# A two-layer diffusion backbone on one core: MLP products in single PSUM banks taken in turn, dot products spread over both MLP products, two of four weight sums added by an accumulating DMA

## The chip, the cores and the metric

The kernel runs on one core of one Trainium2 chip. The time is the device time of one execution in microseconds (us), and lower is better. The core's engines are TensorE (PE, the matrix products, with PEld for its weight loads), VectorE (DVE), ScalarE (ACT), GpSimd (POOL) and SyncE (SP), which here only issues DMA transfers. TensorE writes its products into PSUM, which holds eight banks of 512 fp32 columns on 128 partitions; DVE and ACT read them from there.

## The reference, cut to what matters

```python
def sq_relu_mlp(h, w1, w2):
    return jnp.square(jax.nn.relu(h @ w1)) @ w2

def reference(...):
    h = ctx                                   # 256 context tokens; x: 512 latent tokens
    for l in range(2):
        mod_x = jax.nn.silu(c) @ w_ada[l] + b_ada[l]         # adaLN rows, 6 * 1024
        mod_c = jax.nn.silu(c_ctx) @ w_ada[l] + b_ada[l]
        ...                                                  # retention, attention, pooling
        x = x + g2 * sq_relu_mlp(modulate(rmsnorm(x, norm_mlp[l]), sh2, sc2), w_ff1[l], w_ff2[l])
        if not last:
            h = h + cg2 * sq_relu_mlp(modulate(rmsnorm(h, norm_mlp[l]), csh2, csc2), w_ff1[l], w_ff2[l])
    return rmsnorm(x, norm_final)
```

The model width is 1024, the MLP's inner width 4096. Everything is fp32. The change touches the MLP of both layers and, through it, the place of the adaLN products of layer 1.

## The kernel before

**Tokens and precision.** Activations lie transposed: features on the 128 partitions, tokens along the columns. Layer 0 has 768 columns (512 latent and 256 context tokens), layer 1 512 (latent alone). A matrix product is made of three matmuls on rounded parts (`mm3`, L206: high by high, high by low, low by high). So each 512-column piece of a weight is split after its load: ACT writes the rounded high part (L214), DVE the rest (L223). Both go into a tile `wt`. Pieces are split four ahead of the product that uses them.

**The MLP** is `layer_ff`. The inner width is cut into chunks, 8 in layer 0 and 4 in layer 1. A chunk has two stages. In the *ups*, columns of `w_ff1` give products `f` that ACT takes out of PSUM, with relu and square, into tiles `b` (L1409). DVE builds sums `T` of them (L1363, L1364) and splits all into tiles `act`. In the *downs*, blocks of `w_ff2` are multiplied by these. Except in the last chunk of a layer, the downs use the Strassen-Winograd scheme: of a block's four quarters A11, A12, A21 and A22 and their four sums S1 to S4, seven are multiplied by one activation tile each, in the order A11, S1, A12, S4, S3, S2, A22. A chunk has two such blocks in layer 0 (a product there has two output halves i = 0, 1 of 128 features with 6 matmuls each) and four in layer 1 (one output, 12 matmuls). The four sums are made by DVE out of the loaded quarters (`quarter`, L250), 128 by 512 elements each:

```python
a, b = {S1: (A21, A22), S2: (S1, A11), S3: (A11, A21), S4: (S2, A12)}[i]
```

There are 26 such blocks in the program: 2 in each of seven chunks of layer 0, 4 in each of three of layer 1. The last chunk of a layer is a plain product.

**What takes a product out of PSUM.** DVE, in two ways: `keep` adds it to a tile `V` in SBUF (L1363), `gate` multiplies it by the adaLN gate and adds it to the residual `x` (L1453). A11 needs both, S1, S3 and S2 a `keep`, A12, S4 and A22 gates.

**PSUM.** `psum(3, 2)` makes three tiles A of two banks each and two single banks B. In layer 0 each up and each product takes a whole tile A, so three are in flight, and a tile is free again when the last read of both its halves is done. In layer 1 `bank` hands out halves of the tiles A, so six products are in flight. The two banks B serve small products.

**The dots.** Part of the adaLN rows of layer 1 is not computed on PE: rows of the transposed `w_ada` (`w_adaT`, 256 KB each) are multiplied by the conditioning vector and summed by DVE instructions of 128 by 512 (L474, output and input `rows`; one or two for each load). 96 such loads belong to layer 0's MLP, spread over chunks 0 to 6, about 14 each. They are merged into the list of ups alone, not among the downs. Chunk 0 has more of this kind among its ups: 8 more row loads and a piece of layer 0's adaLN on PE (matmuls `ada<-rows`).

**What sets the order.** `layer_ff` writes a list of tasks, `emit` walks it: it starts the load of a weight 3 units, and that of a `rows` tile 8 tasks, before its use. All these loads stand in one row on the SP queue, and each waits there until its buffer is free: 4 buffers of 4 KB per partition for weights (a block of `w_ff2` takes two) and `N_RR` = 3 buffers for rows. Then a scheduler places the instructions of each engine; an engine runs its own in that order.

Of the kernel before, what the change touches and what calls it, by code (L numbers as in the profile page):

```python
# [15 lines left out]
P = 128  # L16
# [46 lines left out]
N_RR = 3  # L63
# [27 lines left out]
class Unit:  # L91
# [55 lines left out]
class Net:  # L147
    def __init__(self, nc, tc, es, a):
# [9 lines left out]
        self.ps = self.half = None  # L158
        self.es = es
# [82 lines left out]
    def quarter(self, u, i):  # L242

        if i < 4:
            return u.raw[i // 2][:, i % 2 * 512:i % 2 * 512 + 512]
        if i not in u.sums:
            a, b = {S1: (A21, A22), S2: (S1, A11), S3: (A11, A21), S4: (S2, A12)}[i]
# [1070 lines left out]
    def layer_ff(self, l, whole, groups):  # L1318
# [32 lines left out]
        def begin():  # L1351
            n = per * 2 // 4
            t = [self.d("V", F32).rearrange("p a t -> p (a t)") for _ in range(-(-3 // n))]
            for i, name in enumerate("U57"):
                st[name] = [t[i // n][:, (i % n * 4 + j) * hw:(i % n * 4 + j + 1) * hw] for j in range(4)]
                st[name, "all"] = t[i // n][:, i % n * 4 * hw:(i % n + 1) * 4 * hw].rearrange("p (j t) -> p j t", t=hw)
# [61 lines left out]
        def up(c, m, u):  # L1418
            if last:
                ps = self.bank("f1")  # L1420
                self.lin1(ps, u, H, NK, 0, w)
                evac(c, m, None, [(ps, 0, w)])
                return
            ps = self.A("f1", (P, 2, 512))
            for half in range(2):
                o = half * hw
                for k in range(NK):
                    s = slice(k * P, (k + 1) * P)
                    self.mm3(ps[:, half, :hw], u[:, 0, s], u[:, 1, s], H(k)[:, 0, o:o + hw], H(k)[:, 1, o:o + hw], k == 0, k == NK - 1)
                evac(c, m, half, [(ps[:, half, :hw], o, hw)])  # L1430
# [26 lines left out]
        def keep(c, blk, name, ps):  # L1457
            v = st[name, "all"][:, MP * blk:MP * blk + MP]
            if c == 0 and (name, blk) not in st:
                st[name, blk] = True  # L1460
# [4 lines left out]
        def gates(blk, ps, odd, half):  # L1465
            for i in range(MP):
                gate(2 * (MP * blk + i) + odd, half, ps[:, i, :], bool(odd))

        use = {A11: (B11, lambda c, j, ps: (keep(c, j, "U", ps), gates(j, ps, 0, 0))),
               S1: (T1, lambda c, j, ps: keep(c, j, "5", ps)),  # L1470
               A12: (B21, lambda c, j, ps: gates(j, ps, 0, 0)),
               S4: (B22, lambda c, j, ps: gates(j, ps, 0, 1)),
               S3: (T3, lambda c, j, ps: keep(c, j, "7", ps)),
               S2: (T2, lambda c, j, ps: keep(c, j, "U", ps)),
               A22: (T4, lambda c, j, ps: gates(j, ps, 1, 0))}

        def product(c, u, blk, name):
            q, f = use[name]
            ps = self.bank("f2")[:, None, :hw] if last else self.A("f2", (P, 2, 512))[:, :, :hw]
            t = u.pieces[name].t  # L1480
            for i in range(MP):
                for p in range(CP):
                    s = slice((i * CP + p) * P, (i * CP + p + 1) * P)
                    self.mm3(ps[:, i, :], t[:, 0, s], t[:, 1, s], *part(c, p, q), p == 0, p == CP - 1)
            f(c, blk, ps)

        def block(c, blk, u):
            cost = 3 * 4 * hw / 2.2
            return [Task(cost, lambda n=n: product(c, u, blk, n), (u.pieces[n],))
                    for n in (A11, S1, A12, S4, S3, S2, A22)]  # L1490
# [34 lines left out]
        for c in range(n_chunk):  # L1525
# [13 lines left out]
            extra = self.extra.pop(("ff1", l), []) if c == 0 else []  # L1539
# [202 lines left out]
```

## Time and profile before

| | us |
|---|---|
| median of 3 runs | 1658.56 (1658.44 to 1662.48) |
| the profiled execution | 1657.6 |
| its span in the trace | 1655.8 |
| PE busy in the span | 1552.9 (94%) |
| DVE busy | 1183.5 (71%) |
| ACT busy | 802.4 (48%) |

The profiled execution's time is 1.8 us longer than the span that its trace shows, and 1.0 us under the median. Busy times are those of one engine, and the engines work beside each other. In the rows further down, a number in square brackets is the time for which the engine stood idle before an instruction, with the instruction that ended this wait; PEclk is the clock that TensorE was granted, as a share of its full speed.

### The profile page before, as it was taken

Reading aid. Unit: us, or ns where it says so; the run is one execution under the profiler, and the core shown is the slowest. Engines: PE = TensorE matmul, PEld = TensorE weight load, DVE = VectorE, ACT = ScalarE, POOL = GpSimd, SP = SyncE. Lnnn points to the kernel's source line nnn. Section 1 sums busy time; section 2 is a strip of 40 time slices with the busy share of each in tenths; the row PEclk is TensorE's granted clock in tenths of the full one; section 3 lists DMA queues with packets and bytes.
Section 4 is the critical chain, followed back from the end, with each engine's and each line's share of the span. In section 5 each row is a group of like instructions: output and inputs, shape, how many; then the busy total and the mean of one; then the engine's idle time right before and its main releaser. Section 6 shows DMA issues by size and latency. Waiting matters only on the chain.

```text
span 1655.8 us, 24510 instructions
## 1 busy us (share of the span) xinstructions
PE 1552.9 (94%) x9100; PEld 1351.4 (82%) x9100; DVE 1183.5 (71%) x2564; ACT 802.4 (48%) x1635; POOL 38.2 (2%) x78
## 2 busy tenths in 40 slices
PE   5999999999869898999999998998999999999997
PEld 2898577878659798899988997976888788888976
DVE  5665756877787979779787948678556785867834
ACT  4425477545334343434434345267764655445443
POOL 0010000000000000000000000101000000000000
PEclk8999999999879899999999999999999999999999
DMA  9352545652433234332432231723433223242321
GB/s 368 112 150 64 148 103 127 193 188 84 128 114 109 96 108 133 116 121 96 131 112 84 88 109 63 208 80 86 101 103 121 77 89 103 71 121 73 119 89 51
DMA packets 69095, 191.98 MB, mean 116 GB/s; under 512 B 8944, under 2 KB 11504, under 8 KB 68976
## 3 DMA queue, kind: packets, MB, share of 16 engines
q1 hardware_dynamic: 65584, 180.18, 34.7%
q0 software_dynamic: 2816, 9.70, 2.6%
q8 instruction: 72, 1.18, 0.3%
q10 hardware_dynamic: 576, 0.52, 0.1%
q14 instruction: 47, 0.39, 0.1%
HBM read 159.97 MB, written 10.49 MB: 103 GB/s over the span
## 4 chain that ended last, share of the span: by engine, by line
PE 84%; DVE 10%; DMA 3%; ACT 3%; issue 1%; SPq 0%; DVEq 0%; ACTq 0%
PE f L206 48%; PE A L206 10%; PE sc L206 4%; PE oe L206 3%; PE pv L206 3%; PE res L206 3%; PE rv L206 2%; PE pT L1031 2%; PE ada L206 2%; DVE act L223 1%; DVE rows L474 1%; PE ro L206 1%; DMA rows<-w_adaT 1%; PE q L206 1%; DVE dot L474 1%; DMA raw<-w_ada 1%
## 5 line engine op out<-in xcount | busy, mean ns | idle before, releaser
L206 PE MATMUL f<-h,wt 128*128 128x384 f32 (+2 forms) x2400 | 466.9, 355 | 10.3 <-ACT b L1409 7.7
L206 PE MATMUL f<-act,wt 128*128 128x256 f32 (+2 forms) x2664 | 436.1, 324 | 41.2 <-DVE x L1453 15.3
L206 PEld LDWEIGHTS f<-h,wt 128*128 128x128 f32 x2400 | 419.9, 191 | 54.3 <-ACT b L1409 14.2
L206 PEld LDWEIGHTS f<-act,wt 128*128 128x128 f32 x2664 | 411.5, 195 | 64.1 <-DVE x L1453 17.2
L223 DVE TENSOR_TENSOR wt<-raw,wt 128x512 fp32r<-128x512 f32 x326 | 222.0, 687 | 150.5 <-ACT wt L214 148.1
L214 ACT ACTIVATE wt<-raw 128x512 fp32r<-128x512 f32 x326 | 201.4, 627 | 228.1 <-PE f L206 124.9
L206 PE MATMUL A<-h,wt 128*128 128x512 f32 (+2 forms) x864 | 171.9, 357 | 1.0 <-ACT h L554 0.5
L206 PEld LDWEIGHTS A<-h,wt 128*128 128x128 f32 x864 | 143.0, 190 | 27.5 <-ACT h L554 2.8
L214 ACT ACTIVATE wt<-sum 128x512 fp32r<-128x512 f32 x104 | 63.0, 628 | 154.2 <-DVE sum L250 143.0
L1409 ACT ACTIVATE b<-f 128x384 f32<-128x384 f32 (+2 forms) x98 | 50.5, 518 | 149.5 <-PE f L206 135.0
L206 PE MATMUL sc<-k,q 96*128 96x512 f32 (+1 forms) x384 | 85.5, 350 | 2.6 <-ACT p L1013 1.9
L474 DVE SCALAR_TENSOR_TENSOR rows<-rows,sbc 128x512 f32<-128x512 f32 x128 | 84.4, 686 | 1.9 <-DMA rows<-w_adaT 1.4
L206 PEld LDWEIGHTS sc<-k,q 96*128 96x128 f32 x384 | 62.8, 188 | 20.4 <-issue 5.5
L1363 DVE TENSOR_TENSOR V<-V,f 128x768 f32<-128x768 f32 (+1 forms) x86 | 62.5, 726 | 21.6 <-PE f L206 21.4
L223 DVE TENSOR_TENSOR wt<-sum,wt 128x512 fp32r<-128x512 f32 x104 | 70.6, 686 | 7.5 <-ACT wt L214 7.3
L1453 DVE SCALAR_TENSOR_TENSOR x<-f,mod,x 128x256 f32<-128x256 f32 (+2 forms) x148 | 68.9, 503 | 6.5 <-PE f L206 4.7
L1012 DVE TENSOR_REDUCE st<-sc 128x1 f32<-128x768 f32 x64 | 60.7, 953 | 15.1 <-PE sc L206 14.7
L1032 ACT ACTIVATE pT<-pT 128x384 f32<-128x384 f32 x128 | 56.5, 491 | 22.4 <-PE pT L1031 22.0
L214 ACT ACTIVATE act<-T 128x384 fp32r<-128x384 f32 (+1 forms) x104 | 47.6, 472 | 38.9 <-DVE T L1364 19.5
L223 DVE TENSOR_TENSOR act<-b,act 128x384 fp32r<-128x384 f32 (+2 forms) x94 | 47.5, 515 | 25.0 <-ACT act L214 24.9
L206 PE MATMUL res<-mix,wt 128*128 128x256 f32 (+1 forms) x384 | 59.1, 313 | 2.3 <-DVE om L1052 1.9
L1013 ACT ACTIVATE p<-sc,st 128x768 f32<-128x768 f32 x64 | 57.8, 905 | 5.6 <-DVE st L1012 4.4
(244 smaller groups left out, 1849.6 us busy)
## 6 DMA issues: line engine op xcount, KB each, us to landing
raw<-w_ff SPq DMA_DIRECT2D x128, 512.0 KB, 3.6
rows<-w_adaT SPq DMA_DIRECT2D x128, 256.0 KB, 3.0
raw<-w_in SPq DMA_DIRECT2D x22, 512.0 KB, 4.1
raw<-w_ada SPq DMA_DIRECT2D x16, 512.0 KB, 10.9
rows<-w_ada SPq DMA_DIRECT2D x32, 256.0 KB, 3.1
raw<-w_out SPq DMA_DIRECT2D x16, 512.0 KB, 3.7
x<-xd SPq DMA_DIRECT2D x6, 768.0 KB, 6.8
x<-xT SPq DMA_DIRECT2D x4, 768.0 KB, 6.5
```

The costliest lines, as they stand in the source:

```text
L206: self.nc.tensor.matmul(out, l, r, start=start, stop=stop)
L214: self.nc.scalar.activation(out, src, AF.Copy, **k)
L223: return self.nc.vector.tensor_tensor(out, src, hi.bitcast(F32), op=ALU.subtract)
L474: nc.vector.scalar_tensor_tensor(out, w, 1.0, self.sbc[:, v, half], op0=ALU.mult, op1=ALU.mult, accum_out=acc[:, v, i, j:j + 1])
L1012: nc.vector.tensor_reduce(st[:, 0:1], ps, axis=AX, op=ALU.max, negate=True)
L1013: nc.scalar.activation(p, ps, AF.Exp, bias=st[:, 0:1], accum_out=st[:, 1:2])
L1031: nc.tensor.transpose(ps[:, kt, :], p[:, (k0 + kt) * P:(k0 + kt + 1) * P], self.ident)
L1032: nc.scalar.activation(s["pT", h, qt // 2][:, k0:k0 + 3, c], ps, AF.Copy)
L1363: add = lambda x, y, z, op=ALU.add: nc.vector.tensor_tensor(x, y, z, op=op)
L1409: nc.scalar.activation(b[:, at:at + n], ps, AF.Relu)
L1453: self.mark = nc.vector.scalar_tensor_tensor(x, ps[:, at - o:at - o + n], g[:, cond:cond + 1], x, op0=ALU.mult, op1=ALU.add)
```

## The change

Four things change.

1. **Banks.** `bank` hands out all eight banks in turn: the two halves of a tile A, a bank B, two halves, a B, two halves. Ups and products of both layers take one bank for each half (`up`) or for each output half i (`product`). A product of layer 0 becomes two tasks, and its `keep` two additions of 128 by 384 in place of one of 128 by 768.
2. **Sums.** The order of the quarters in `w_ff2` becomes A21, A22, A11, A12. A block is loaded by three DMAs on the SP queue in place of two: A21 twice, side by side into the tile `sums` (512 KB written), A11 and A12 into `raw` (512 KB), and A22 into half a tile `rh` (256 KB, two buffers). Then a DMA on the POOL queue adds A22 and A11, from HBM, to what lies in `sums` (512 KB): the tile then holds S1 and S3. DVE makes S2 and S4 alone. In a plain chunk A21 is loaded once and nothing is added.
3. **Dots.** They are merged into ups and downs together; in chunk 0 among the downs alone, since its ups keep the other rows.
4. **Room.** `N_RR` goes from 3 to 2, the descriptor memory of software DMAs from 4096 to 2048.

```diff
 def bank(self, name):
-    if self.half is None:
+    i = self.turn
+    self.turn = (i + 1) % 8
+    if i in (2, 5):
+        return self.B([P, 512], name)
+    if i in (0, 3, 6):
         self.half = self.A(name, (P, 2, 512))
         return self.half[:, 0, :]
-    t, self.half = self.half, None
-    return t[:, 1, :]
+    return self.half[:, 1, :]
...
 def load_unit(self, u):
         if u.kind == "st":
-            u.raw = [self.wr.tile([P, UW], F32, tag="r", name=self.nm("raw")) for _ in range(2)]
-            for i in range(2):
-                q.dma_start(u.raw[i], u.ap[:, i * 1024:i * 1024 + 1024])
+            u.raw = [self.wr.tile([P, UW], F32, tag="r", name=self.nm(n)) for n in ("sums", "raw")]
+            u.raw.append(self.wr.tile([P, 512], F32, tag="rh", name=self.nm("raw"), bufs=2))
+            r = u.raw[0].rearrange("p (a c) -> p a c", a=2)
+            if u.plain:
+                q.dma_start(r[:, 0, :], u.ap[:, 0:512])
+            else:
+                q.dma_start(r, u.ap[:, None, 0:512].to_broadcast([P, 2, 512]))
+            q.dma_start(u.raw[1], u.ap[:, 1024:2048])
+            q.dma_start(u.raw[2], u.ap[:, 512:1024])
+            if not u.plain:
+                self.nc.gpsimd.dma_start(u.raw[0], u.ap[:, 512:1536], accum_op=ALU.add)
             return
...
-            a, b = {S1: (A21, A22), S2: (S1, A11), S3: (A11, A21), S4: (S2, A12)}[i]
+            a, b = {S2: (S1, A11), S4: (S2, A12)}[i]
...
-        def product(c, u, blk, name):
+        def product(c, u, i, j, name):
             q, f = use[name]
-            ps = self.bank("f2")[:, None, :hw] if last else self.A("f2", (P, 2, 512))[:, :, :hw]
+            ps = self.bank("f2")[:, :hw]
             t = u.pieces[name].t
-            for i in range(MP):
-                for p in range(CP):
-                    s = slice((i * CP + p) * P, (i * CP + p + 1) * P)
-                    self.mm3(ps[:, i, :], t[:, 0, s], t[:, 1, s], *part(c, p, q), p == 0, p == CP - 1)
-            f(c, blk, ps)
+            for p in range(CP):
+                s = slice((i * CP + p) * P, (i * CP + p + 1) * P)
+                self.mm3(ps, t[:, 0, s], t[:, 1, s], *part(c, p, q), p == 0, p == CP - 1)
+            f(c, j, ps)
...
-            extra = self.extra.pop(("ff1", l), []) if c == 0 else []
             share = -(-len(spread) // max(n_chunk - 1 - c, 1))
-            extra, spread = extra + spread[:share], spread[share:]
-            out += merge(ups, extra)
...
+            extra, spread = spread[:share], spread[share:]
+            if c == 0:
+                out += merge(ups, self.extra.pop(("ff1", l), []))
+                out += merge(downs, extra)
+            else:
+                out += merge(ups + downs, extra)
```

How the order moves is shown at three places. The first is PE at the start of the downs of layer 0's chunk 3, just after the last up. `f_1196` is the product A11, `f_1198` S1, `f_1202` A12 and `f_1204` S4; a row with x3 is three matmuls. Before:

```order
L206 MATMUL f_1196_6697<-act_6514,wt_6532 128x384
L206 MATMUL f_1198_6716<-act_6394,wt_6537 128x384 x3
L206 MATMUL f_1198_6716<-act_6598,wt_6537 128x384 x3
L206 MATMUL f_1198_6716<-act_6394,wt_6537 128x384 x3
L206 MATMUL f_1198_6716<-act_6598,wt_6537 128x384 x3
L206 MATMUL f_1202_6737<-act_6474,wt_6608 128x384 x3
L206 MATMUL f_1202_6737<-act_6598,wt_6608 128x384 x3
L206 MATMUL f_1202_6737<-act_6474,wt_6608 128x384 x3
L206 MATMUL f_1202_6737<-act_6598,wt_6608 128x384 x3
L206 MATMUL f_1204_6755<-act_6474,wt_6615 128x384 x3
L206 MATMUL f_1204_6755<-act_6675,wt_6615 128x384 x3
```

Now, from the same place on: `f_1199` is A11 (its second output half comes after the first of S1), `f_1202` and the second half of `f_1203` belong to S1, `f_1207` to A12, `f_1209` to S4, `f_1212` to S3 and `f_1214` to S2.

```order
L211 MATMUL f_1202_6735<-act_6617,wt_6556 128x384 x3
L211 MATMUL f_1203_6743<-act_6423,wt_6556 128x384 x2
L211 MATMUL f_1199_6712<-act_6423,wt_6553 128x384 x3
L211 MATMUL f_1199_6712<-act_6544,wt_6553 128x384 x3
L211 MATMUL f_1203_6743<-act_6423,wt_6556 128x384
L211 MATMUL f_1203_6743<-act_6617,wt_6556 128x384 x3
L211 MATMUL f_1207_6766<-act_6503,wt_6625 128x384 x3
L211 MATMUL f_1207_6766<-act_6617,wt_6625 128x384 x3
L211 MATMUL f_1209_6777<-act_6503,wt_6632 128x384 x3
L211 MATMUL f_1212_6799<-act_6537,wt_6709 128x384 x3
L211 MATMUL f_1212_6799<-act_6692,wt_6709 128x384 x3
L211 MATMUL f_1214_6818<-act_6537,wt_6732 128x384 x3
```

PE now goes through first halves of A12, S4, S3 and S2 before it comes back to the second halves; no product waits for the bank of A11 before six other half products are through.

The second place is DVE at the same point. `V` takes the kept product, `T` and `act` serve the last up, `rows` are dots, `wt` splits of weights. Before, from the addition of A11 to its second gate (`x_730`):

```order
L1363 TENSOR_TENSOR V_4294<-V_4294,f_1196_6697 128x768
L1363 TENSOR_TENSOR T_6674<-b_6643,b_6565 128x384
L223 TENSOR_TENSOR act_6675<-b_6643,act_6675 128x384
L1364 SCALAR_TENSOR_TENSOR T_6596<-T_6596,b_6643 128x384
...
L250 TENSOR_TENSOR sum_6692<-raw_6335,raw_6336 128x512
L223 TENSOR_TENSOR act_6682<-T_6674,act_6682 128x384
L474 SCALAR_TENSOR_TENSOR rows_6602,acc_6522<-rows_6602,sbc 128x512
L474 SCALAR_TENSOR_TENSOR rows_6605,acc_6522<-rows_6605,sbc 128x512
L223 TENSOR_TENSOR wt_6694<-sum_6692,wt_6694 128x512
...
L1453 SCALAR_TENSOR_TENSOR x_730_3780<-f_1196_6697,mod_155,x_730_3780 128x384
```

Now:

```order
L1376 TENSOR_TENSOR V_4295<-V_4295,f_1199_6712 128x384
L1461 SCALAR_TENSOR_TENSOR x_729_3779<-f_1199_6712,mod_155,x_729_3779 128x384
L488 SCALAR_TENSOR_TENSOR rows_6623,acc_6705<-rows_6623,sbc 128x512
L1376 TENSOR_TENSOR T_6691<-b_6660,b_6583 128x384
...
L1376 TENSOR_TENSOR V_4295<-V_4295,f_1199_6712 128x384
L228 TENSOR_TENSOR act_6699<-T_6691,act_6699 128x384
L488 SCALAR_TENSOR_TENSOR rows_6551,acc_6705<-rows_6551,sbc 128x512
L1461 SCALAR_TENSOR_TENSOR x_730_3780<-f_1199_6712,mod_155,x_730_3780 128x384
L228 TENSOR_TENSOR wt_6732<-sum_6628,wt_6732 128x512
```

The first gate now follows its addition at once, the sum of this stretch is gone, and the last row, the split of S2's weights, stands behind the second gate.

The third place is DVE in layer 1, where the third block of a chunk begins. Before, the four sums of the block (`raw_13762`, `raw_13763` are its loads):

```order
L250 TENSOR_TENSOR sum_13925<-raw_13763 128x512
L1363 TENSOR_TENSOR V_12399<-V_12399,f_2354_13946 128x256
L250 TENSOR_TENSOR sum_13960<-sum_13925,raw_13762 128x512
L223 TENSOR_TENSOR wt_13927<-sum_13925,wt_13927 128x512
L1363 TENSOR_TENSOR V_12401<-V_12401,f_2350_13911 128x256
L223 TENSOR_TENSOR wt_13943<-raw_13762,wt_13943 128x512
L250 TENSOR_TENSOR sum_13962<-sum_13960,raw_13762 128x512
L1453 SCALAR_TENSOR_TENSOR x_2078_12069<-f_2354_13946,ng_12833,x_2078_12069 128x256
L250 TENSOR_TENSOR sum_13980<-raw_13762,raw_13763 128x512
```

Now (`sums_13844` is the third block's tile of sums, which the DMA adds to; rows with 13663 to 13665 and the `sum_13914`, `sum_13916` belong to the block before):

```order
L264 TENSOR_TENSOR sum_13914<-sums_13663,raw_13664 128x512
L1461 SCALAR_TENSOR_TENSOR x_2097_12146<-f_2363_13921,ng_12916,x_2097_12146 128x256
L1376 TENSOR_TENSOR V_12477<-V_12477,f_2358_13884 128x256
L264 TENSOR_TENSOR sum_13916<-sum_13914,raw_13664 128x512
L264 TENSOR_TENSOR sum_14043<-sums_13844,raw_13845 128x512
L1376 TENSOR_TENSOR V_12477<-V_12477,f_2363_13921 128x256
L228 TENSOR_TENSOR wt_13918<-sum_13916,wt_13918 128x512
L228 TENSOR_TENSOR wt_13935<-sums_13663,wt_13935 128x512
```

The first sum of the third block, which reads the DMA's result, stands ahead of the splits of S4 (`wt_13918`) and S3 (`wt_13935`) of the second block and ahead of additions of its products.

## Rows read from the trace of the kernel before

**Rows 1.** The page's busy times: us, share of the span, instructions.

```profile
PE 1552.9 (94%) x9100; PEld 1351.4 (82%) x9100; DVE 1183.5 (71%) x2564; ACT 802.4 (48%) x1635; POOL 38.2 (2%) x78
```

**Rows 2.** Windows of layer 0's chunks 0 to 3; chunk 3 also by ups and downs.

```profile
core 0: us, PE busy (x) PEld busy (x) DVE busy (x) ACT busy (x) POOL busy (x), PEclk, DMA share, GB/s
405.40:512.00 106.60, 86.49 (x437) 73.55 (x438) 85.95 (x214) 40.80 (x82) 0.00 (x0) 0.86 0.37 115
512.00:587.90 75.90, 68.02 (x362) 65.01 (x361) 63.51 (x145) 27.74 (x52) 0.00 (x0) 0.93 0.32 102
587.90:657.20 69.30, 64.48 (x362) 61.99 (x361) 56.42 (x123) 27.84 (x52) 0.00 (x0) 1.00 0.36 113
657.20:693.10 35.90, 35.90 (x204) 35.49 (x204) 23.18 (x55) 16.31 (x31) 0.00 (x0) 1.00 0.42 134
693.10:726.10 33.00, 29.15 (x159) 28.83 (x158) 31.66 (x59) 11.90 (x21) 0.00 (x0) 0.95 0.32 97
657.20:726.10 68.90, 65.05 (x361) 64.32 (x361) 54.85 (x114) 28.21 (x52) 0.00 (x0) 0.98 0.37 116
```

**Rows 3.** Timeline of PE where chunk 3's downs begin: start, length, operation.

```profile
688.89 4.40 PE L206 MATMUL f<-h,wt 128*128 128x384 f32 x24
693.13 4.58 PE L206 MATMUL f<-act,wt 128*128 128x384 f32 x25
701.56 4.61 PE L206 MATMUL f<-act,wt 128*128 128x384 f32 x16 [3.85 <-DVE x L1453]
```

**Rows 4.** Timeline of DVE in the same stretch.

```profile
693.51 0.95 DVE L1363 TENSOR_TENSOR V<-V,f 128x768 f32<-128x768 f32 x1 [2.45 <-PE f L206]
...
697.32 0.69 DVE L250 TENSOR_TENSOR sum<-raw,raw 128x512 f32<-128x512 f32 x1
...
700.89 0.62 DVE L1453 SCALAR_TENSOR_TENSOR x<-f,mod,x 128x384 f32<-128x384 f32 x1
```

**Rows 5.** Window right after that wait, columns as in rows 2.

```profile
702.20:705.40 3.20, 3.20 (x11) 3.20 (x11) 3.20 (x6) 0.00 (x0) 0.00 (x0) 0.50 0.47 117
```

**Rows 6.** DVE's groups in chunk 3: busy us, mean ns, idle time before.

```profile
L474 DVE SCALAR_TENSOR_TENSOR rows<-rows,sbc 128x512 f32<-128x512 f32 x14 | 9.1, 686 | 0.0
L1363 DVE TENSOR_TENSOR V<-V,f 128x768 f32<-128x768 f32 x8 | 7.6, 952 | 3.3 <-PE f L206 3.3
...
L250 DVE TENSOR_TENSOR sum<-sum,raw 128x512 f32<-128x512 f32 x4 | 2.7, 687 | 0.0
...
L1364 DVE SCALAR_TENSOR_TENSOR T<-T,b 128x384 f32<-128x384 f32 x4 | 2.2, 553 | 0.0
```

**Rows 7.** Timeline of PE in chunk 0, three of its waits.

```profile
446.31 1.91 PE L206 MATMUL ada<-rows,sc 128*32 128x512 f32 x2 [2.33 <-DMA rows<-w_ada]
...
471.31 6.97 PE L206 MATMUL f<-h,wt 128*128 128x384 f32 x24 [7.03 <-ACT b L1409]
...
488.21 23.92 PE L206 MATMUL f<-act,wt 128*128 128x384 f32 x120 [3.42 <-ACT wt L214]
```

**Rows 8.** DMA issues: count, KB each, median us from issue to landing.

```profile
raw<-w_ff SPq DMA_DIRECT2D x128, 512.0 KB, 3.6
rows<-w_adaT SPq DMA_DIRECT2D x128, 256.0 KB, 3.0
...
QQ<-rope POOLq DMA_DIRECT2D x8, 192.0 KB, 7.0
...
q<-q POOLq DMA_DIRECT2D x4, 384.0 KB, 4.5
```

**Rows 9.** Timeline of PE in layer 1, second chunk, around its one wait.

```profile
1427.09 0.51 PE L206 MATMUL f<-act,wt 128*128 128x256 f32 x2 [1.12 <-ACT wt L214]
1428.03 35.75 PE L206 MATMUL f<-act,wt 128*128 128x256 f32 x286 [0.43 <-DVE wt L223]
```

**Rows 10.** Timeline of DVE at that place.

```profile
1425.69 0.68 DVE L250 TENSOR_TENSOR sum<-raw,raw 128x512 f32<-128x512 f32 x1
```

**Rows 11.** Window of layer 1, rest of the second chunk's downs and the next ups.

```profile
1432.00:1513.00 81.00, 81.00 (x491) 71.29 (x490) 57.13 (x120) 40.37 (x79) 0.00 (x0) 1.00 0.31 94
```

More of the change, by code (lines that the diff above doesn't have):

```diff
@@ L62 @@
 RA = 8
-N_RR = 3
+N_RR = 2
 N_DP = 22
@@ L96, in __init__ @@
     def __init__(self, ap, w, kind=None, queue=None):
-        self.ap, self.w, self.kind, self.queue = ap, w, kind, queue
+        self.ap, self.w, self.kind, self.queue, self.plain = ap, w, kind, queue, False
         self.raw, self.sums = None, {}
@@ L158, in __init__ @@
         self.ps = self.half = None
+        self.turn = 0
         self.es = es
@@ L242, in quarter @@
     def quarter(self, u, i):
-        if i < 4:
-            return u.raw[i // 2][:, i % 2 * 512:i % 2 * 512 + 512]
+        if i not in (S2, S4):
+            t, o = {A21: (0, 0), S1: (0, 0), S3: (0, 1), A11: (1, 0), A12: (1, 1), A22: (2, 0)}[i]
+            return u.raw[t][:, o * 512:o * 512 + 512]
         if i not in u.sums:
-            a, b = {S1: (A21, A22), S2: (S1, A11), S3: (A11, A21), S4: (S2, A12)}[i]
+            a, b = {S2: (S1, A11), S4: (S2, A12)}[i]
             a, b = self.quarter(u, a), self.quarter(u, b)
@@ L1418, in up @@
         def up(c, m, u):
-            if last:
+            for half in (None,) if last else range(2):
+                o, n = (half * hw, hw) if half is not None else (0, w)
                 ps = self.bank("f1")
[L1421 to L1426, printed above, removed]
                 for k in range(NK):
                     s = slice(k * P, (k + 1) * P)
-                    self.mm3(ps[:, half, :hw], u[:, 0, s], u[:, 1, s], H(k)[:, 0, o:o + hw], H(k)[:, 1, o:o + hw], k == 0, k == NK - 1)
-                evac(c, m, half, [(ps[:, half, :hw], o, hw)])
+                    self.mm3(ps[:, :n], u[:, 0, s], u[:, 1, s], H(k)[:, 0, o:o + n], H(k)[:, 1, o:o + n], k == 0, k == NK - 1)
+                evac(c, m, half, [(ps[:, :n], o, n)])
         def up_two(us):
@@ L1455, in gate, with keep @@
             self.gated = self.gated[-1:] + [self.mark]
[L1457 to L1460, printed above, removed]
+        def keep(c, j, name, ps):
+            v = st[name][j]
+            if c == 0 and (name, j) not in st:
+                st[name, j] = True
                 nc.scalar.activation(v, ps, AF.Copy)
@@ L1502, in plain @@
         def plain(c, u, blk, i, odd, gs):
+            self.turn = 0
             ps = self.A("f2")
@@ L1538, in layer_ff @@
                 ups = merge(ups, [Task(1, lambda j=j: finish(j)) for j in range(4)])
-            extra = self.extra.pop(("ff1", l), []) if c == 0 else []
-            share = -(-len(spread) // max(n_chunk - 1 - c, 1))
-            extra, spread = extra + spread[:share], spread[share:]
-            out += merge(ups, extra)
             blocks = [Unit(a["w_ff2"][l, c * n_blk + blk], 2048, "st") for blk in range(n_blk)]
+            for u in blocks:
+                u.plain = c == n_chunk - 1
+            downs = []
             if c < n_chunk - 1:
                 for blk in range(n_blk):
-                    out += block(c, blk, blocks[blk])
+                    downs += block(c, blk, blocks[blk])
+            share = -(-len(spread) // max(n_chunk - 1 - c, 1))
+            extra, spread = spread[:share], spread[share:]
[4 more added lines that the diff above has]
+                out += merge(ups + downs, extra)
         out.append(Task(0, self.stat_start))
@@ L1636, in _quarters @@
     t = t.transpose(0, 4, 3, 6, 2, 5, 1, 7).reshape(16, P, 2, 2, 512)
[L1637 removed]
+    return np.stack([t[:, :, 1, 0], t[:, :, 1, 1], t[:, :, 0, 0], t[:, :, 0, 1]], axis=2).reshape(16, P, 2048)
 def _rope_tables(length, dim):
@@ L1736 @@
     arrays = _prepare(inputs)
-    nc = _bacc.Bacc("TRN2", target_bir_lowering=False, num_devices=1, dynamic_dma_scratch_size=4096)
+    nc = _bacc.Bacc("TRN2", target_bir_lowering=False, num_devices=1, dynamic_dma_scratch_size=2048)
     program(nc, arrays)
```

19 lines of the change are left out of this document (7 added, 12 removed).

## The prediction, made before the changed kernel ran

> **What bounds the kernel now.** I read the busy times first: PE is busy for 94% of the span, DVE for 71% [rows 1]. That says PE is the bound on the whole; it doesn't say where a change can gain. So I cut layer 0's MLP into its chunks. Of chunk 3's 68.9 us PE is idle 3.85 and has a mean clock of 0.98 [rows 2]. The timeline shows one wait: the last up's 24 matmuls take 4.40 us (0.18 each), the downs begin at 693.13, and after two products PE stands from 697.71 to 701.56, released by DVE's `x` [rows 3]. That is the fourth product in need of the PSUM tile of the first, A11, whose second gate ends at 700.89 + 0.62 = 701.51. DVE got A11 at 693.51 and put the last up's sums and splits, a weight sum and two dots ahead of that gate [rows 4]. Right after it the clock is at 0.50 for 3.2 us [rows 5], the lower of the two levels, which costs half of that, 1.6. Chunks 4 to 6 repeat this with waits of 3.8 to 3.85 and have 68.4 to 68.7 us; so the loss is 4 times 5.4.
>
> Inside the downs PE isn't far from DVE: 29.15 us against 31.66 busy in 33.0, while in the ups DVE has 23.18 in 35.9 [rows 2]. Chunk 0 is worse: 106.6 us, PE 86.49, DVE 85.95, clock 0.86; chunk 1 has 75.9 us and clock 0.93 [rows 2]. Chunk 0's waits are many and for several things: `ada` rows from HBM (2.33), ups' outputs `b` (7.03, the tile again), weights (3.42) [rows 7]. Layer 1 takes six banks in turn already; each of its three Strassen chunks has one wait, such as 1.12 + 0.43, where a sum that DVE makes at 1425.69 comes late to ACT's and DVE's splits of it [rows 9, 10].
>
> **The banks (layer 0).** A product gives its bank back per half. Eight banks instead of three tiles: A11's banks are wanted again only by S3, one product later than now: 12 matmuls, 2.1 us. Ahead of A11's second gate stand a sum less (0.69) and one dot less (0.69) [rows 4, 6]. That is 3.5 of the 3.85, so of this wait some 0.35 is left, too short to take the clock down as 3.85 did. But the order of DVE shows the split of S2's weights behind that gate, while PE wants them as the seventh half product, of 1.06 us each; I charge 0.9 per chunk for both. Chunks 3 to 6: 4 x (5.4 - 0.9) = **-18** (bounds -22 and -9: all of it, and somewhat under half). Chunk 2 (69.3 us, without the low clock) goes to what chunk 3 would need, 64.3: **-5**.
>
> **DVE's work.** Two sums of 26 blocks go: 52 x 0.687 = 35.7 us [rows 6]. `keep` is cut in two: 8 additions of 0.952 in a chunk become 16 of 128 by 384; the trace has none of these from PSUM, and the nearest row has 0.553 [rows 6], 16 x 0.553 - 7.6 = +1.2. A chunk of layer 0 thus loses 4 x 0.687 - 1.2 = 1.5 of DVE time. This alone buys nothing where PE is the bound; it pays for the dots in the downs.
>
> **The dots.** A chunk's 14 dots (9.1 us with 0.686 each [rows 6]) spread over both stages: about half stay with the ups, whose DVE has 12.7 us free. DVE's downs: 31.66 with the dots that the scheduler already lets slip there, less 2.7 of sums, plus 1.2, plus perhaps 3: about 33 where PE needs 29.2, so DVE lags some 4 us by a chunk's end. Eight banks hold that: PE can be seven half products ahead, 7 x 6 x 0.18 = 7.4 us. Chunk 1 has 28 dots and lags some 9, which leaves a wait of 2. There I expect of the 75.9 - 64.3 = 11.6 us that could be had two thirds, **-8** (bounds -11.6 and 0).
>
> In chunk 0 the spread dots go to the downs alone. Its ups are rid of 14 loads and their dots in the row of the SP queue and on DVE, which shortens the waits for `ada` rows and for `b`; but the `rows` tiles are two in place of three, and a load that lands after 3.0 us [rows 8] holds its buffer for two dots, 1.4. The downs get all 28 dots, 19.2 us on DVE, beside 28 of its own, where PE needs 29.2: 47 us, so some 10 us of wait for DVE come back there. The floor of the whole chunk is DVE's 85.95 - 1.5 = 84.5, so the gain lies between 22 and 0; I take the middle, **-12**, since the 7.03 and 3.42 go with the banks and the waits in the downs come new.
>
> **The loads and the accumulating DMA.** A block costs the SP queue three loads of 512, 512 and 256 KB for two of 512, and POOL's queue 512 KB. DMA is busy 0.37 of the time in chunk 3 [rows 2]; 26 blocks with 0.75 MB more are 20 MB over two layers' MLPs, which the engines have room for. What counts is the delay. The trace has no accumulating transfer. Bounds: 3.6 us, as a plain load of that size, and 18.7, POOL's worst row scaled by size (7.0 x 512 / 192); I take 6.0, from POOL's other row (4.5 x 512 / 384), since both move rows of kilobytes [rows 8]. It starts when the first load has landed, so S1 is there 3.6 + 6.0 = 9.6 us after the buffer comes free. In layer 0 blocks are loaded while the ups run, 15 us and more ahead, and POOL is idle: nothing lost. In layer 1 a product of 12 matmuls takes 1.5 us (286 in 35.75 [rows 9]) and a block 10.5. The third and fourth blocks' buffers come free when the first and second are split to the end, about a block before their first sum stands on DVE: 7.5 to 10 us by the order. Behind that sum wait, on DVE, splits of S4 and S3 of the block before and additions that free PSUM, which PE needs about 3 us later. 9.6 lands inside this: a wait of DVE up to 2 us, none of PE. The three waits of layer 1 (2.1, 1.55 as in [rows 9], and 1.56) come with some 1.6 of clock each, 10 us at most; a late sum is their cause [rows 10], and two sums fewer help, so I take **-6** (bounds -10 and +20, below).
>
> The Trainium skill prices a transfer of this queue ("DMA: Bandwidth & Descriptors", section "Anatomy of one DMA — SWDGE (gpsimd) path") at about 2.0 us plus bytes over 436 GB/s; as an estimate from that page, 512 KB take 3.2 us. By it the sums would be there three microseconds sooner and the forecast would not change; no run here shows whether it holds for an addition.
>
> **Two row buffers.** In the stages of retention and attention the rows' loads have one buffer less. PE's waits for them are few now; if each pair of dots must end before the next load begins, they may show: **+3** (bounds 0 and +8).
>
> **The sum**, against the profiled execution's 1657.6: -18 - 5 - 8 - 12 - 6 + 3 = -46, so **1612 us** on the profile's scale; the median of the runs is 1 us higher, which I leave inside the range.
>
> **The rivals.** *DVE takes the place of the banks.* With dots in the downs, DVE needs 33 us where PE needs 29; if its order lets evacuation wait behind dots and splits as it does now [rows 4], chunks 0 to 2 give nothing and chunks 3 to 6 keep half of 4 x 5.4: -11 - 6 + 3, so 1644, with 1626 to 1650 as its own range. For it speaks that 31.66 of 33.0 is nearly full; against it, that chunk 3's downs have one wait, at their start, and none where the lag of DVE would be longest.
>
> *The addition is late (the other side).* Place: the first sum of layer 1's third and fourth blocks. Order and cushion allow the transfer about 8 us (11.6 with the first load). Each microsecond more comes twice in each of three chunks, 6 us in all. Without layer 1's 6 us the gain is 40, so from about 15 us on the kernel is slower, and at 18.7 it is 10.7 x 6 = 64 later, at 1682. For it: nothing in the trace shows such a transfer, and POOL's row of 192 KB took longer than that of 384. Against: it moves the bytes of a plain load that takes 3.6.
>
> *Banks in turn lower the clock.* If PE, paced by DVE, makes a short stop at each half product, the clock could stay at 0.50 as in [rows 5]; for all of chunk 0's and 1's downs and a third of the five next that is 2 x 29 + 5 x 10 = 108 us at half speed, which loses 54. Of these, 20 are lost now too (0.86 of 106.6 and 0.93 of 75.9 us), and the forecast wins some 6 of them back: 40 more than forecast, 1652. The Trainium skill describes this ("TensorE: Matmul & The Clock Gate", section "A second HAM failure mode: psum-queue depth-cycling"): cycling through PSUM banks makes PE stop briefly between groups, and the clock swings between its levels. Here the trace disagrees so far: layer 1 cycles through six banks with the clock at 1.00 over 81 us [rows 11].
>
> *More than forecast.* Chunks 0 to 2 reach the floor: -22 - 11.6 - 5, 1597 or less.
>
> **How the numbers follow.** Forecast (1598 to 1625) 0.55; DVE the bound (1626 to 1650) 0.19; more than forecast 0.07; clock (about 1652) 0.07; late addition 0.12. The first two and the better one's upper end hold 0.8: the range is 1592 to 1648; the forecast's own is 1598 to 1625. A measurement of this kernel tells 0.3%, 5 us, from no change: faster 0.83 (the first three and 0.02 of the clock's), same 0.06 (0.05 of the clock's and 0.01 of the late addition's), slower 0.11.
>
> **What would show it.** Right: no wait of PE on `x` after two products of chunks 3 to 6, the clock at 1.00 there, chunks of 64 to 65 us; DVE's sums 52 (of 104) and no PE wait that ends by `sums`; chunk 0 near 95, chunk 1 near 68. Wrong: PE waits on DVE `V` or `x` within the downs; `sum <- sums` on DVE idle for the DMA for over 3 us; clock below 0.95 in chunks 2 to 6; waits on `rows` that grow in chunk 0 or in attention.

## The result, and the profile of the changed kernel

The changed kernel takes 1637.9 us in the median (1633.7 to 1642.1), before 1658.5 in the same comparison; the ratio is 0.9877, with a 95% interval from 0.9835 to 0.9918. So it got faster by some 21 us where 46 were forecast. The time lies inside the stated range of 1592 to 1648, far from its middle, and outside the forecast's own of 1598 to 1625. The rows below are of an execution of 1634.5 us, one of the two shorter of four.

The busy times, which answer to [rows 1]:

```profile
PE 1544.9 (95%) x9100; PEld 1331.9 (82%) x9100; DVE 1155.3 (71%) x2562; ACT 798.1 (49%) x1641; POOL 60.9 (4%) x104
```

DVE lost 28 us; worked out were 35.7 of sums less 7 times 1.2 for the halved additions, 27. The windows of layer 0's chunks 0 to 4, columns as in [rows 2]:

```profile
411.07:498.27 87.20, 77.19 (x418) 62.66 (x419) 72.39 (x184) 39.74 (x86) 0.91 (x1) 0.96 0.44 130
498.27:571.51 73.24, 66.99 (x362) 63.27 (x362) 63.70 (x160) 26.47 (x51) 1.74 (x2) 0.98 0.48 141
571.51:640.33 68.82, 65.73 (x367) 62.61 (x367) 58.21 (x135) 28.72 (x54) 1.73 (x2) 1.00 0.48 136
640.33:706.00 65.67, 63.27 (x354) 60.98 (x355) 51.74 (x113) 26.95 (x51) 1.75 (x2) 1.00 0.53 147
706.00:773.69 67.69, 65.44 (x367) 62.96 (x367) 53.80 (x119) 28.20 (x54) 1.76 (x2) 1.00 0.50 140
```

Chunk 0 is shorter by 19.4 us, chunks 1 and 2 by 2.7 and 0.5, chunks 3 and 4 by 3.2 and 0.7 (a chunk is counted from its first up, which slips a little into the chunk before). The low clock behind the wait is gone. The wait is smaller but there. The start of chunk 4's downs on PE, which answers to [rows 3]:

```profile
742.97 5.52 PE L211 MATMUL f<-act,wt 128*128 128x384 f32 x30
748.76 1.32 PE L211 MATMUL f<-act,wt 128*128 128x384 f32 x6 [0.28 <-DVE x L1461]
751.52 1.31 PE L211 MATMUL f<-act,wt 128*128 128x384 f32 x6 [1.43 <-DVE x L1461]
```

PE does 30 matmuls and stands: five half products, that is, five output halves of 6 matmuls each. Then it does one more and stands again. One more wait, of 0.45, follows before the downs end. DVE in the same downs, three rows of its timeline for the gates of A11's two halves (`x_729`, then `x_730`) and the next addition, which answer to [rows 4], and the window of the downs:

```profile
748.10 0.61 DVE L1461 SCALAR_TENSOR_TENSOR x<-f,mod,x 128x384 f32<-128x384 f32 x1
...
750.85 0.61 DVE L1461 SCALAR_TENSOR_TENSOR x<-f,mod,x 128x384 f32<-128x384 f32 x1
...
751.45 0.55 DVE L1376 TENSOR_TENSOR V<-V,f 128x384 f32<-128x384 f32 x1
```

```profile
747.40:773.70 26.30, 24.06 (x134) 22.48 (x133) 25.82 (x59) 7.14 (x12) 0.00 (x0) 1.00 0.40 121
```

DVE is busy for 25.82 of 26.30 us while PE has waits: by the look of it DVE has become the bound there. The new transfers, count, KB each and us to landing, which answer to [rows 8]:

```profile
sums<-w_ff SPq DMA_DIRECT2D x26, 512.0 KB, 4.2
sums<-w_ff POOLq DMA_DIRECT2D x26, 512.0 KB, 7.4
```

The addition takes 7.4 us where I took 6.0, inside the bounds of 3.6 and 18.7. In layer 1 it lands late. DVE's timeline at the second chunk's fourth block, and PE there, which answer to [rows 9, 10]:

```profile
1422.91 0.69 DVE L264 TENSOR_TENSOR sum<-sums,raw 128x512 f32<-128x512 f32 x1 [3.79 <-DMA sums<-w_ff]
```

```profile
1424.98 5.29 PE L211 MATMUL f<-act,wt 128*128 128x256 f32 x22 [2.48 <-DVE wt L228]
```

DVE waits for additions four times, 10.0 us in all; PE waits behind them 1.28, 2.82 and 2.48. Summed up by stretches of the trace (the last column is a kernel of the second set of experiments):

| stretch | forecast | changed kernel | with one-bank tiles (e5) |
|---|---|---|---|
| start of layer 0's MLP | +3 | +5.7 | +7.0 |
| its chunk 0 | -12 | -19.4 | -21.5 |
| chunk 1 | -8 | -2.7 | -9.3 |
| chunk 2 | -5 | -0.5 | -6.3 |
| chunks 3 to 6 | -18 | -8.3 | -24.8 |
| chunk 7 to layer 1's MLP | 0 | +4.4 | +3.2 |
| layer 1's MLP to the end | -6 | -2.4 | -14.6 |
| sum of the spans | -46 | -23.1 | -66.3 |

Of the +4.4, 1.8 is only where chunk 7's first up begins; the rest lies in layer 1's attention stage, a window of which has a clock of 0.97 where it had 1.00. No run was made for that.

### The profile page after: what moved, and what is told of

Same layout as the page of the kernel before. It is cut to its first block, busy times and chain, and to the rows that moved or that the text cites. A ratio compares the mean times of both kernels' runs of the same rounds, so it can differ in the third digit from the quotient of the medians.

```text
span 1632.7 us, 24664 instructions
## 1 busy us (share of the span) xinstructions
PE 1544.9 (95%) x9100; PEld 1331.9 (82%) x9100; DVE 1155.3 (71%) x2562; ACT 798.1 (49%) x1641; POOL 60.9 (4%) x104
## 4 chain that ended last, share of the span: by engine, by line
PE 53%; DVE 13%; DMA 3%; ACT 2%; issue 1%; DVEq 0%; POOLq 0%; ACTq 0%; SPq 0%
PE f L211 37%; PE A L211 4%; DMA sums<-w_ff 2%; DVE wt L228 2%; PE sc L211 2%; DVE x L1461 2%; DVE V L1376 2%; PE oe L211 1%; DVE rows L488 1%; PE pv L211 1%; PE pT L1045 1%; PE rv L211 1%; PE res L211 1%; DVE sum L264 1%; DVE act L228 1%
## 5 line engine op out<-in xcount | busy, mean ns | idle before, releaser
L211 PE MATMUL f<-h,wt 128*128 128x384 f32 (+2 forms) x2400 | 460.5, 351 | 4.5 <-DVE x L1461 1.8
L211 PEld LDWEIGHTS f<-h,wt 128*128 128x128 f32 x2400 | 413.3, 189 | 47.6 <-ACT b L1422 5.3
L211 PEld LDWEIGHTS f<-act,wt 128*128 128x128 f32 x2664 | 398.0, 191 | 64.1 <-DVE x L1461 25.5
L219 ACT ACTIVATE wt<-raw 128x512 fp32r<-128x512 f32 (+1 forms) x320 | 199.3, 629 | 282.3 <-PE f L211 166.7
L228 DVE TENSOR_TENSOR wt<-raw,wt 128x512 fp32r<-128x512 f32 (+1 forms) x320 | 218.2, 687 | 134.5 <-ACT wt L219 133.0
L488 DVE SCALAR_TENSOR_TENSOR rows<-rows,sbc 128x512 f32<-128x512 f32 x128 | 86.6, 684 | 0.4
L1376 DVE TENSOR_TENSOR V<-V,f 128x384 f32<-128x384 f32 (+1 forms) x136 | 68.7, 512 | 12.3 <-PE f L211 11.9
L219 ACT ACTIVATE wt<-sum 128x512 fp32r<-128x512 f32 x52 | 32.6, 627 | 73.5 <-DVE sum L264 55.5
L211 PE MATMUL oe<-mix,wt 128*128 128x512 f32 (+1 forms) x288 | 60.6, 363 | 0.0
L211 PEld LDWEIGHTS res<-mix,wt 128*128 128x128 f32 x384 | 53.1, 189 | 8.2 <-DVE om L1066 2.8
```

The lines of the kernel that those rows point to most:

```text
L211: self.nc.tensor.matmul(out, l, r, start=start, stop=stop)
L219: self.nc.scalar.activation(out, src, AF.Copy, **k)
L228: return self.nc.vector.tensor_tensor(out, src, hi.bitcast(F32), op=ALU.subtract)
L488: nc.vector.scalar_tensor_tensor(out, w, 1.0, self.sbc[:, v, half], op0=ALU.mult, op1=ALU.mult, accum_out=acc[:, v, i, j:j + 1])
L1376: add = lambda x, y, z, op=ALU.add: nc.vector.tensor_tensor(x, y, z, op=op)
```

## First set of experiments: the parts of the change

Three theories stood against each other: A, that of the forecast; B, that DVE is the bound of the downs; C, that the addition lands late in layer 1. Each kernel is a part of the change's own diff; the diffs shown are cut to what matters.

**e1**, the banks alone (against the changed kernel):

```diff
-N_RR = 2
+N_RR = 3
...
-                self.nc.gpsimd.dma_start(u.raw[0], u.ap[:, 512:1536], accum_op=ALU.add)
...
+            out += merge(ups, extra)
...
-                out += merge(ups + downs, extra)
```

> Before with the eight banks alone (sums all on DVE, dots in the ups, three row buffers). Theory A, that of the forecast (three PSUM tiles are what holds the downs up): chunks 3 to 6 of layer 0 lose their wait of 3.85 us and the low clock behind it, 64 to 65 us each, and the time is about 1636 us. Theory B (DVE is the bound of the downs): DVE has 31.7 us of work in the downs plus 1.2 for the halved additions, where PE needs 29.2; PE waits of 2 to 3 us a chunk stay, spread over the downs, chunks of 66 to 67 us, and the time is about 1645. Layer 1 as before in both.

Measured: 1649.0 us against 1656.9 (ratio 0.9952, 0.9938 to 0.9965). PE at the start of chunk 4's downs:

```profile
755.79 5.52 PE L210 MATMUL f<-act,wt 128*128 128x384 f32 x30
763.92 1.31 PE L210 MATMUL f<-act,wt 128*128 128x384 f32 x6 [2.61 <-DVE x L1451]
```

Theory A's number is missed by 13, and B is the nearer. But the rows show more: after five half products PE is stopped by the first gate of A11 (763.26 to 763.86 on DVE), so it cannot be seven ahead.

**e2**, the accumulating DMA alone, with two row buffers, on the tiles and the dots of before (the other part of the diff: `load_unit`, `quarter`, the order of `w_ff2`, `N_RR`).

> Before with the accumulating DMA alone (and the two row buffers that make room for it): PSUM tiles and dots as before. Theory A: A11's wait shrinks by the one sum ahead of its gate, to about 3 us, and the low clock stays: 4 to 5 us less in layer 0, 3 us lost to the row buffers, about 1657. Theory B: 2.7 us of DVE work less in each chunk of layer 0 come off the end of the downs, 7 x 2.7 = 19, less the row buffers' 4: about 1643. Theory C (the addition lands late in layer 1): chunks 0 and 1 of layer 1 have waits of 1 to 3 us on DVE work that stands behind a sum, layer 1 no better than before.

Measured: 1685.4 us (ratio 1.0162, 1.0139 to 1.0185). A's and B's numbers are both missed by over 25; C named none. In the profiled run, at 1676.6 the shortest of five, layer 0's MLP starts 5.3 us later, its chunk 0 is 6 longer (PE waits for `ada` rows 8.4 us in four pieces, where it had two, 2.43 and 2.33), and chunk 0 of layer 1 is 4 longer, with waits of 2.18 and 3.09 on DVE. That is C's mechanism and the row buffers'; what makes the other runs some 9 us longer than the profiled one, no trace shows.

**e3**, banks and dots without the addition (three row buffers).

> The change without the accumulating DMA: eight banks and spread dots, all four sums on DVE, three row buffers. Theory A: as the changed kernel but for the row buffers, 1632 to 1636. Theory B: each chunk's downs get 2.7 us of sums back on a DVE that is full there, so PE waits 2 to 3 us longer in chunks 0 to 6: 1650 to 1655. Theory C: layer 1 gets 2 to 4 us shorter than in the changed kernel.

Measured: 1638.0 us (ratio 0.9883, 0.9865 to 0.9902), the changed kernel's time to a tenth. A's number (1632 to 1636) is missed by 2, B's (1650 to 1655) by 12. The dots are worth 11.0 here (e1 less e3). Chunk 0 goes from 104.6 to 86.6, but chunks 1 to 6 together from 412.8 to 423.5: with all sums on DVE the dots in the downs do cost, as B says. By C layer 1 should be shorter than the changed kernel's: from its MLP's start to the end it is 373.2 against 375.3.

**e4**, the changed kernel with the dots among the ups:

```diff
+            out += merge(ups, extra)
...
-                    downs += block(c, blk, blocks[blk])
...
-            if c == 0:
-                out += merge(ups, self.extra.pop(("ff1", l), []))
-                out += merge(downs, extra)
-            else:
-                out += merge(ups + downs, extra)
+                    out += block(c, blk, blocks[blk])
```

> The changed kernel with the dots back among the ups alone, in chunk 0 too. Theory A: the downs don't care; chunk 0 is as long as before, some 15 to 19 us longer than in the changed kernel, the rest equal: about 1655. Theory B: DVE has 3 to 4 us less in each of the downs of chunks 1 to 6, PE's waits of 2 to 5 us there go: 12 to 18 us less, chunk 0 gives 15 to 19 back: about the changed kernel's 1638, with another profile.

Measured: 1664.8 us (ratio 1.0055, 1.0038 to 1.0073), more than either theory said (1655 and 1638). Chunk 0 has 112.5 us, 25 more than in the changed kernel. Chunks 1 to 6 together have 410.3 against 408.3, so with two sums fewer, taking the dots out of the downs won nothing, and B's forecast fails here.

## Second set: tiles of one bank, and the row buffers

e1 and e4 sent me to the trace with the program's list beside it. A tile A holds two banks, and `bank` gives its halves to two half products that follow each other. The list of PE's instructions in the changed kernel, with what they wait for, for the two halves of one such tile (S1 of chunk 4's first block, between them other products):

```
L211 MATMUL f_1291_7364<-act_7052,wt_7185 128x384 x3
...
L211 MATMUL f_1291_7364<-act_7052,wt_7185 128x384 [waits DVE_49]
```

The second half waits for DVE, though it lies in another bank and its operands have been used already. In the trace the first half is written from 745.20, DVE adds it to `V` from 751.45 to 752.00, and the second begins at 752.32. I paired all matmuls and reads of layer 0's downs with the list: of 60 such tiles in chunks 1 to 6 of the changed kernel, in all 60 the second half begins after DVE's last read of the first, by a median of 0.33 us, and 5.9 us after the end of the first half. So the tile, not the bank, is what is waited for. The list also tells which banks PE's two marked waits in chunk 4 are for. The first, of 0.28, stands before S4's second half. That half goes into the bank of the last up, which ACT had read by 743.66; but the same tile holds A11's first half, and PE goes on at 748.76, after A11's gate ends at 748.71. The second, of 1.43, stands before S3's second half, which wants the bank of A11's second half itself. So A11 holds PE up when five half products are done, A11's own two among them, and not only after the six others that were counted where the new order was shown. Theory D: that coupling holds up the downs.

**e5**, the changed kernel with eight tiles of one bank from chunk 0's downs to the last chunk's ups, in both layers:

```diff
-        self.pa = self.ps.enter_context(self.tc.tile_pool(name=self.nm("pa"), bufs=na, space=PSUM))
+        self.single = na == 0
+        if na:
+            self.pa = self.ps.enter_context(self.tc.tile_pool(name=self.nm("pa"), bufs=na, space=PSUM))
...
 def bank(self, name):
+        if self.single:
+            return self.B([P, 512], name)
...
                 out += merge(ups, self.extra.pop(("ff1", l), []))
+                out.append(Task(0, lambda: self.psum(0, 8)))
                 out += merge(downs, extra)
...
+        out.append(Task(0, lambda: self.psum(3, 2)))
         out.append(Task(0, self.stat_start))
```

> The changed kernel with eight PSUM tiles of one bank each for the downs and the ups between, in place of three tiles of two banks and two of one. Theory D (the second half of a two-bank tile is written only after DVE's read of the first, so that five half products can be owed and not seven): the waits of PE for x and V in the downs of chunks 1 to 6, 2 to 6 us each, go almost wholly; 12 to 15 us less than the changed kernel, 1623 to 1626, chunks 3 to 6 at 64 us. Theory B (DVE, busy for 25.8 of 26.3 us of the downs, sets their pace whatever the banks): no more than 3 us less, 1635 to 1638.

Measured: 1590.9 us (ratio 0.9594, 0.9577 to 0.9612), 47 less than the changed kernel. D's direction is right and its size, 12 to 15, too small: in the traces chunks 1 to 6 win 28.8, and layer 1, which D did not name, 12.2. PE's timeline through all of chunk 4, and the windows of chunks 1 to 3 and of chunk 4's downs:

```profile
689.57 33.44 PE L215 MATMUL f<-h,wt 128*128 128x384 f32 x192
722.85 29.28 PE L215 MATMUL f<-act,wt 128*128 128x384 f32 x168
751.97 3.28 PE L215 MATMUL f<-h,wt 128*128 128x384 f32 x18
```

```profile
497.40:564.00 66.60, 64.44 (x361) 62.25 (x361) 64.22 (x162) 26.43 (x52) 1.74 (x2) 1.00 0.53 156
564.00:627.10 63.10, 62.89 (x363) 62.20 (x361) 55.84 (x131) 27.61 (x53) 1.73 (x2) 1.00 0.51 148
627.10:689.60 62.50, 62.50 (x361) 62.50 (x362) 53.06 (x117) 27.66 (x52) 1.75 (x2) 1.00 0.52 154
722.90:752.00 29.10, 29.10 (x170) 29.10 (x169) 27.91 (x64) 11.10 (x20) 0.00 (x0) 1.00 0.39 127
```

No wait is left in chunk 4: 192 matmuls of ups and 168 of downs in one go, 62.4 us a chunk. And DVE is nearly as full as before, 27.91 of 29.10. So a full DVE did not set the pace; it only had no slack to be late in, as long as PE could not run ahead.

**e6**, the same tiles without the addition, with three row buffers.

> Eight tiles of one bank and spread dots, all sums on DVE, three row buffers. Theory D: the waits of 2.5 to 4 us in the downs go here too as long as a chunk's whole DVE work is less than PE's: 12 to 16 us less than the kernel with two-bank tiles, 1622 to 1626, so that the accumulating DMA is worth nothing. Theory B: 2.7 us of sums more for DVE in each of the downs keep PE waiting, 1635 or more.

Measured: 1597.8 us (ratio 0.9641, 0.9624 to 0.9658), 40 less than e3 with two-bank tiles; both theories expected much more time. Chunks 3 to 6 have 63.9 to 64.7: here the sums cost 2 us a chunk, B's cost again, once the pairs are gone.

**e7**, e3 with `N_RR = 2`:

> Eight banks and spread dots, all sums on DVE, but two row buffers in place of three. If the row buffers are what delays the start of layer 0's MLP in the changed kernel: that start comes 5 to 6 us later than with three, chunk 0 up to 1 later, 1643 to 1645. If it is the loads or the addition, no difference: 1638.

Measured: 1645.3 us (ratio 0.9933, 0.9917 to 0.9948), 7.3 more than e3; layer 0's MLP starts at 411.68 in place of 405.33, and chunk 0 is 2.0 longer. So the row buffers, not the loads, delay the start.

**e8**, e5 with the addition in layer 0 alone:

```diff
-            if not u.plain:
+            if u.acc:
                 self.nc.gpsimd.dma_start(u.raw[0], u.ap[:, 512:1536], accum_op=ALU.add)
...
+                u.acc = l == 0 and c < n_chunk - 1
```

> The kernel with eight tiles of one bank, the addition kept in layer 0 alone; layer 1's four sums are all on DVE, out of the same three loads (A21 once). Theory C (the addition, 7 to 8 us, lands late in layer 1): the waits of 1.3, 2.8 and 2.5 us behind late sums in layer 1's chunks 0 and 1 go, 3 to 5 us less than with the addition in both. If those waits have another cause, DVE's 24 more sums make it no shorter: 0 to 2 us longer.

Measured: 1591.4 us (ratio 0.9602, 0.9585 to 0.9619), the same as e5. With one-bank tiles the late addition costs nothing. In layer 1 of e5 DVE waits for it even longer than in the changed kernel, three times and 13.0 us in all, up to 5.6, and PE's timeline marks no wait on DVE in those downs: PE has enough in hand.

## Third set: how much is depth, and the best of all

**e9**, e5 with five tiles of one bank, three banks idle:

```diff
-                out.append(Task(0, lambda: self.psum(0, 8)))
+                out.append(Task(0, lambda: self.psum(0, 5)))
```

> The kernel with one-bank tiles of run e5, but five of them in place of eight (three banks idle). Theory D1 (a two-bank tile that takes its second half only after the first is read acts as one, so three pairs and two singles are worth about five banks): about the changed kernel's time, 1625 to 1640, with waits of 2 to 4 us in each of the downs. Theory D2 (depth is not it; what costs is that PE must take halves out of turn, or that one read of two halves frees a pair late): five single banks are about as good as eight, 1592 to 1605.

Measured: 1612.5 us (ratio 0.9729, 0.9713 to 0.9746), between the two. PE in chunk 4's downs, its only two waits:

```profile
739.84 1.31 PE L215 MATMUL f<-act,wt 128*128 128x384 f32 x6 [0.43 <-DVE x L1465]
742.59 23.65 PE L215 MATMUL f<-act,wt 128*128 128x384 f32 x132 [1.44 <-DVE x L1465]
```

Five separate banks are 25 us better than three pairs and two singles, and the other three are worth 22 more. Of the 25, 12.2 are in chunks 1 to 6 and 11.3 in layer 1, where five do about as well as eight (364.0 against 363.1). So a pair is worth less than one bank of its own. Where the time goes in chunks 3 to 6 suggests why. Counted against e5's 0.173 us a matmul, the first 12 us of the four downs lose 7.4 us in the changed kernel and 8.2 in e9; the rest of the chunks loses 9.1 and 1.9. The five banks run short once, at the start of the downs, and the coupling of the pairs comes again. A pair couples in two ways, the second half behind the read of the first, and the whole tile kept until both are read; no run separates them.

**e10**, before with products in halves on one-bank tiles and nothing else (e1 with e5's diff).

> Before with eight PSUM tiles of one bank each for the downs and the ups between, and nothing else: no addition by DMA, dots in the ups, three row buffers. If the forecast's term for the banks was right but for the tiles: chunks 3 to 6 go from 68.7 to 64 us or less, chunk 2 by 5, chunk 1 by 8, layer 1 by 6, and chunk 0 stays over 100: 1605 to 1615. If the banks need the dots moved or the sums taken off DVE to be worth anything: 1635 or more.

Measured: 1607.1 us (ratio 0.9694, 0.9676 to 0.9713). Chunks 3 to 6 have 62.8 to 63.6 us, chunk 2 63.9, chunk 1 69.4, chunk 0 still 100.2. So single banks alone are worth 50 us, where e1's pairs gave 8, and nothing of the other parts is needed for it. Layer 1 is 13.7 shorter than before with all four sums on DVE; PE in its second chunk, ups and downs, where before it waited 1.12 and 0.43 [rows 9]:

```profile
1332.20 45.15 PE L214 MATMUL f<-h,wt 128*128 128x512 f32 x192
1377.19 40.15 PE L214 MATMUL f<-act,wt 128*128 128x256 f32 x336
```

The wait is gone with no sum taken away, so it was not the late sum that made it: with pairs it stays (e1 has 2.09, 1.25 and 2.10 in the three chunks). One wait of PE in chunk 0, for an up's output, shows that chunk 0's loss is another:

```profile
469.52 11.24 PE L214 MATMUL f<-act,wt 128*128 128x384 f32 x48 [11.95 <-ACT b L1416]
```

**e11**, e5 with the dots among the ups (e4 with e5's diff).

> The kernel with one-bank tiles of run e5 with the dots back among the ups alone, in chunk 0 too. Chunks 1 to 6 stand at PE's own rate with either place, so nothing changes there; chunk 0 gets its 14 loads and dots back, with two row buffers in the row of the SP queue: 20 to 27 us more, as between e4 and the changed kernel, 1611 to 1618. If the place of the dots matters in the other chunks too, 3 to 6 us less than that.

Measured: 1617.0 us (ratio 0.9755, 0.9739 to 0.9772), 26 more than e5. Chunk 0 has 108.9 against 85.0, chunks 1 to 6 together 383.6 against 379.4.

**e12**, e5 with the third row buffer, paid by one buffer for A22:

```diff
-N_RR = 2
+N_RR = 3
...
-            u.raw.append(self.wr.tile([P, 512], F32, tag="rh", name=self.nm("raw"), bufs=2))
+            u.raw.append(self.wr.tile([P, 512], F32, tag="rh", name=self.nm("raw"), bufs=1))
```

> The kernel with one-bank tiles of run e5 with three row buffers again; the room comes from one buffer in place of two for the single quarter A22. If the row buffers cost what e3 and e7 say (6 us ahead of layer 0's MLP, 1 to 2 in its chunk 0): 1583 to 1585. If a single buffer for A22 holds up the row of the SP queue, waits for weights appear in the downs and eat some of it: 1586 to 1595.

Measured: 1580.4 us (ratio 0.9533, 0.9516 to 0.9550), 10.6 less than e5, some 3 less than expected, and the best of all. Layer 0's MLP starts at 405.65, its chunk 0 has 81.0.

## Why the prediction was wrong, point by point

**The banks: the step that failed.** "Eight banks hold that: PE can be seven half products ahead", and "A11's banks are wanted again only by S3". The terms that rest on it, -18, -5 and -8 for chunks 3 to 6, 2 and 1, came to -8.3, -0.5 and -2.7. The two-bank tile made it five (e1), and the second halves came after the reads of the first all through the downs (60 of 60 tiles). With one-bank tiles the step holds and its terms were even too small: chunks 3 to 6 win 24.8 where 18 were forecast with a floor of 64.3 a chunk, and have 62.4. The sign was in front of the reader: in the order of PE, half products of later products stand ahead of the second halves of earlier ones. I read that as PE having more choice; it was the schedule going around a wait. What an instruction waits for has to be read too. A smaller slip is beside it: "one dot less" was taken to stand ahead of A11's second gate, but the order of DVE has two dots there, now as before; only the sum is gone. That the total fell inside the range all the same is in part luck: chunk 0 gave 7.4 more than its term.

**DVE's work and the dots.** The 28 us of DVE time came close to the 27 worked out. The dots in the downs of chunks 1 to 6 cost nothing where DVE has two sums fewer (e4, e11), and 10.6 us where it makes all four on two-bank tiles (e3 less e1 there). Their gain in chunk 0 was mis-sized: 12 taken, 19.4 measured, near the bound of 22. That bound was none: it took all of DVE's 84.5 us to stay in the chunk, where 72.39 are in it now, and with e12 the chunk has 81.0. Moving them is worth 11 (e1, e3) to 27 us (e4, the changed kernel), and the gain is chunk 0's. The 10 us of DVE waits feared in its downs were some 4, in pieces of 0.2 to 1.0.

**The addition.** 7.4 us in place of 6.0, and late by up to 3.8 on DVE in layer 1, where "a wait of DVE up to 2 us, none of PE" was said; the cushion of about 8 us was not there, since transfers of 7.3 to 7.8 were waited for. PE's waits of 6.6 in all took most of the term of -6. That term had its cause wrong too, a late sum: before's waits in layer 1 go with single banks alone (e10). The new waits were felt only through the tiles: e8 equals e5. The rival of a late addition was right in its place, not in its price. Its worth is 7.4 us in the changed kernel (e7 less this) and 17.4 with one-bank tiles (e6 less e12). The Trainium skill's fit ("DMA: Bandwidth & Descriptors", section "Anatomy of one DMA — SWDGE (gpsimd) path") gives, as an estimate from that page, 3.2 us for these bytes; the trace has 7.4 and that of e5 6.1, so for these additions it is short by about half, and the measurement decides. How much of the difference is other traffic, no run separates.

**The row buffers.** +3 taken, 7.3 measured (e7), inside its bounds.

**The rivals.** DVE as the bound had the time nearly right (1644 against 1638) and the reason wrong. The gains of "more than forecast" add up to 1598, not 1597, and the middle of chunk 0's bounds is 11, not 12; neither changes the account. The swinging clock did not come. The Trainium skill ("TensorE: Matmul & The Clock Gate", section "A second HAM failure mode: psum-queue depth-cycling") describes it for a bf16 kernel that cycles through PSUM banks and idles briefly between groups of matmuls; here the trace disagrees, with a clock of 1.00 in chunks 2 to 6 and, in e5, in chunk 1 as well.

**What stays open.** Why e2's unprofiled runs are 9 us above its profiled one; the 2.7 us in layer 1's attention stage; and how much of the gain of one-bank tiles is the waits themselves and how much the new order that the scheduler writes once they are gone.

## What to carry to other kernels

Before a forecast counts PSUM banks, look at the tile that the program hands out: if two products or halves share a tile, the second's first matmul may wait for the read of the first, and eight banks so paired can be worth less than five separate ones. A full engine beside a waiting one is not yet the bound: give the waiting one room to run ahead and see whether the wait goes. And ask what a change gives up to make room; here one row buffer cost a third of what the whole change brought.

## What the hardware showed that I had not expected

A 512 KB addition by DMA lands 7.4 us after its issue in the changed kernel (6.1 in e5), where a plain load of the same size beside it takes 3.8 to 4.2 (4.1 in e5). And PE keeps 360 matmuls of 384 columns without a gap at 62.4 us, 0.173 each (e5), with DVE busy for 96% of the downs beside it.
